# A planner's cost table changed: charges, a shared port and a settling time for chain matmuls

## The chip, the cores and the metric

The kernel runs on one core of one Trainium2 chip. The metric is the time of one execution on the device in microseconds. Before the change it is 2612.74 us, the median of 3 runs (2610.64 to 2614.07).

## The reference, cut to what matters

A stack of four layers works on 256 latent tokens and 256 context tokens of width 1024. A conditioning vector gives six modulation vectors to each layer. Each layer is a token mixer and then an MLP with squared ReLU (1024 to 4096 to 1024).

- Layers 0 and 3 mix by a gated DeltaNet with 8 heads in both directions: projections, a short convolution, then for each head and direction a triangular inverse and a recurrence over chunks, `o_c = qd_c S + attn_c v_new`, `S = S * cd + kt^T v_new`.
- Layer 1 mixes by a short gated convolution.
- Layer 2 mixes by differential attention with 8 heads: two softmaxes each, the second subtracted with a weight, then the product with v.
- The output is the latent stream after a last RMSNorm. Layer 3 finishes the latent tokens alone.

All is computed in float32. The projections and MLPs split each operand into a high and a low float32r part and add three products (high*high, high*low, low*high).

## The kernel before, in words

All instructions are issued by a planner, class `Issue`, while the program is built; nothing of it runs on the chip. Work is written as generators (`Strand`s). A strand yields either an `Op` (one instruction with its engine, its charge `cost` in ns and a latency `lat` until its result may be read) or a list of things that must be there first (a tile, a free PSUM bank, an event). `run` takes, over and over, the strand whose next step can start first by the planner's clocks (`start`), ties by priority, and `do` issues it: it moves the engine's clock by the charge and notes when the outputs can be read. So the charges set only the order of the instructions on each engine's queue, and in some places which of two engines does a copy (`evac` and `scaled` carry an alternative, `alt`). On the chip each engine runs its queue in that order and waits by semaphores.

Two sorts of matmul share TensorE. The projections' matmuls (`block`, `joint_prod`; kind float32r) read split weights (`whi`, `wlo`) and stream 256 or 512 columns; there are thousands of them, and in the long stretches of the MLPs nothing else runs on TensorE. The chains' matmuls are short: in the DeltaNet layers the transposes and norms of a head (`unit`, `turned`), the decays (`decays`, bf16), the inverse (`inverse`, float16, tile `Z`), the recurrence (`scan`, float32, tiles `S`, `rr`, `vk`, `vn`), and in attention the score, transpose and value products (`diff_probs`, `diff_head`). Between two matmuls of a chain stand VectorE, ScalarE or GpSimd steps. Chains have higher priority than projections, so that projections fill what the chains leave. PSUM has 3 banks for projections (`mm`), 4 for chains (`ch`) and one for outputs (`po`). Heads in flight are bounded by rings of buffers (`RINGS`: in layer 0 two buffers each of `E` and `NT`, in layer 3 three).

A matmul of a chain reaches the planner in one of two ways. The float32, bf16 and transpose ones are mostly yielded as `Op`s. The float16 ones of the inverse (`four`, `four_half`, `sums`), the products into `po` in `scan` and the attention scores are issued by `do` at once when the list before them is met.

During the DeltaNet layers GpSimd takes, beside its part in the chains, the low part of each weight (`splitter`, line 463).

Of the kernel before, what the change touches and what calls it, by code (L numbers as in the profile page):

```python
# [10 lines left out]
F32 = mybir.dt.float32  # L11
F32R = mybir.dt.float32r
F16 = mybir.dt.float16
BF16 = mybir.dt.bfloat16
# [4 lines left out]
PSUM = bass.MemoryType.PSUM  # L19
# [4 lines left out]
T = 256  # L24
TT = 2 * T
NB = TT // P
H = 8
# [4 lines left out]
DH = 64  # L32
LEVELS = 7
HALF = (slice(0, T), slice(T, TT))
LAT = dict(PE=197.0, ACT=150.0, DVE=145.0, POOL=80.0)
BIG = 1e18


class Op:

    __slots__ = ("eng", "cost", "outs", "ins", "emit", "lat", "func", "alt", "pre", "banks")

    def __init__(self, eng, cost, outs, ins, emit, lat, func=None):
        self.eng, self.cost, self.emit, self.lat, self.func, self.alt, self.pre = eng, cost, emit, lat, func, None, 0.0
        self.banks = [] if eng == "PE" else [a.name for a in ins + outs if a.space == PSUM]
        self.outs = [(a.name, Issue.buckets(a)) for a in outs]
        self.ins = [(a.name, Issue.buckets(a)) for a in ins]


class Strand:  # L50
    __slots__ = ("prio", "seq", "gen", "item", "r")
# [13 lines left out]
class Issue:  # L65
# [2 lines left out]

    TABLE = 1283.0
    AHEAD = 50.0  # L70

    def __init__(self, nc):
        self.nc = nc
        self.clk = dict(PE=0.0, ACT=0.0, DVE=0.0, POOL=0.0, DMA=0.0)
        self.rt, self.ft, self.birth, self.rings = {}, {}, {}, {}
        self.tasks, self.seq = [], 0
        self.n = 0
        self.held = set()
        self.loaded = None
        self.pe_begin = 0.0  # L80
        self.bank = {}


    def tile(self, pool, tag, shape, dt=F32, bufs=1, hold=False):
# [87 lines left out]
    def table(self, func):  # L172

        if TABLES[func] != self.loaded:
            self.loaded = TABLES[func]
            self.nc.scalar.preload_act_table_set(self.loaded)  # L176
            self.clk["ACT"] += self.TABLE

    def do(self, op):

        if op.alt is not None and self.clk[op.alt.eng] + op.alt.cost < self.clk[op.eng] + op.cost:
            op = op.alt
        eng = op.eng
        if self.swap_cost(op):
            self.table(op.func)
        begin = max(self.clk[eng], self.ready(op))
        if eng == "PE":
            begin = max(begin, self.pe_begin + op.pre)
            self.pe_begin = begin
        end = begin + op.cost  # L190
        self.clk[eng] = end
        for nm in op.banks:
            self.bank[nm] = (eng, end + op.lat)
        for nm, bs in op.ins:
            f = self.ft[nm]
            for b in bs:
                f[b] = max(f.get(b, 0.0), end)
        for nm, bs in op.outs:
            r = self.rt[nm]
            for b in bs:  # L200
                r[b] = end + op.lat
        op.emit()
# [9 lines left out]
    def mm(self, out, lhsT, rhs, start, stop, **k):  # L212
        n, m = self._n(rhs), self._n(lhsT)
        dt = lhsT.dtype
        if dt == F32R:
            c = n * 0.4167 + 3 if n >= 256 else 215
        elif dt == F32:
            c = n * 1.67 + 5 if n > 64 else 426
        else:
            c = n * 0.4167 + 2  # L220
        op = Op("PE", c, [out], [lhsT, rhs], lambda: self.nc.tensor.matmul(out, lhsT=lhsT, rhs=rhs, start=start, stop=stop, **k), LAT["PE"])  # L221
        op.pre = m * (0.84 if dt in (F32, F32R) else 0.21)
        if k and k["tile_position"][1]:
            op.cost, op.pre = 20, 0.0
        return op

    def transpose(self, out, in_, ident):
        op = Op("PE", 107, [out], [in_, ident], lambda: self.nc.tensor.transpose(out, in_, ident), LAT["PE"])  # L228
        op.pre = 53.0
        return op  # L230

    def act(self, out, in_, func, bias=0.0, scale=1.0, accum_out=None):
# [3 lines left out]
        return Op("ACT", c, [out] + ([accum_out] if accum_out is not None else []), [in_] + ptr,  # L236
                  lambda: self.nc.scalar.activation(out=out, in_=in_, func=func, bias=bias, scale=scale, **k), LAT["ACT"], func)  # L237

    def acopy(self, out, in_):
        return Op("ACT", self._n(in_) / 1.2 + (51 if self._ps(in_) else 93), [out], [in_],  # L240
                  lambda: self.nc.scalar.copy(out=out, in_=in_), LAT["ACT"])  # L241

    def vec(self, n, extra, outs, ins, emit, fast=False):
        ins = [x for x in ins if x is not None and not isinstance(x, float)]
        return Op("DVE", n / (1.92 if fast else 0.96) + extra, outs, ins, emit, LAT["DVE"])

    def vcopy(self, out, in_):
        return self.vec(self._n(in_), 68, [out], [in_], lambda: self.nc.vector.tensor_copy(out=out, in_=in_), not self._ps(in_, out))  # L248

    def vpred(self, out, mask, data):  # L250
        return self.vec(self._n(data), 68, [out], [data], lambda: self.nc.vector.copy_predicated(out=out, mask=mask, data=data))  # L251

    def vtt(self, out, in0, in1, op):
        return self.vec(self._n(in0), 68, [out], [in0, in1], lambda: self.nc.vector.tensor_tensor(out=out, in0=in0, in1=in1, op=op))  # L254
# [17 lines left out]
    def recip(self, out, in_):  # L272
        return Op("DVE", self._n(in_) * 6.3 + 68, [out], [in_], lambda: self.nc.vector.reciprocal(out=out, in_=in_), LAT["DVE"])

# [1 line left out]
        return Op("POOL", n * rate + extra, outs, ins, emit, LAT["POOL"])  # L276

    def ptt(self, out, in0, in1, op):
        return self.pool(self._n(in0), 2.2, 90, [out], [in0, in1],
                         lambda: self.nc.gpsimd.tensor_tensor(out=out, in0=in0, in1=in1, op=op))  # L280

    def psel(self, out, in_, pattern, compare_op, fill, base, cm):
# [17 lines left out]

    def load(self, out, in_):
        n = out.nbytes() if callable(out.nbytes) else out.nbytes
        self.do(Op("DMA", n / 330.0, [out], [], lambda: self.nc.sync.dma_start(out=out, in_=in_), 2000.0))

    def move(self, out, in_):

        n = out.nbytes() if callable(out.nbytes) else out.nbytes
        return Op("DMA", n / 330.0, [out], [in_], lambda: self.nc.sync.dma_start(out=out, in_=in_), 2000.0)


    def spawn(self, gen, prio):
# [27 lines left out]
    def start(self, e):  # L339

        op = e.item
        if not isinstance(op, Op):
            return max(e.r, self.clk["PE"] + self.AHEAD)
        t = self.clk[op.eng]
        if op.alt is not None:
            t = min(t, self.clk[op.alt.eng])
        if op.eng == "PE":
            t += self.AHEAD
        return max(e.r + self.swap_cost(op), t)

    def run(self):
# [23 lines left out]
class Net:  # L375
# [377 lines left out]
    def prod(self, ps, ah, al, bh, bl, first, last):  # L753
        mm = self.I.mm
        yield mm(ps, ah, bh, first, False)
        yield mm(ps, ah, bl, False, False)
        yield mm(ps, al, bh, False, last)
# [1029 lines left out]
```

## Time and profile before

| | |
|---|---|
| Median of 3 runs | 2612.74 us |
| The profiled execution | 2613.07 us, span 2611.4 us |
| TensorE matmul busy | 2515.1 us, 96% |
| TensorE weight load busy | 2091.5 us, 80% |
| VectorE, ScalarE, GpSimd busy | 1899.4, 1257.6, 389.3 us |
| HBM read | 317.44 MB |
| Mean granted clock of TensorE | 0.987 |

Matmuls are pipelined, and the profile models their ends. A busy TensorE can therefore hide short waits: the distance from one matmul's start to the next one's start tells more than the busy time.

### The profile page before, as it was taken

Reading aid. Unit: us, or ns where it says so; the run is one execution under the profiler, and the core shown is the slowest. Engines: PE = TensorE matmul, PEld = TensorE weight load, DVE = VectorE, ACT = ScalarE, POOL = GpSimd, SP = SyncE. Lnnn points to the kernel's source line nnn. Section 1 sums busy time; section 2 is a strip of 40 time slices with the busy share of each in tenths; the row PEclk is TensorE's granted clock in tenths of the full one; section 3 lists DMA queues with packets and bytes.
Section 4 is the critical chain, followed back from the end, with each engine's and each line's share of the span. In section 5 each row is a group of like instructions: output and inputs, shape, how many; then the busy total and the mean of one; then the engine's idle time right before and its main releaser. Section 6 shows DMA issues by size and latency. Waiting matters only on the chain. (4 is left out here: it accounts for less than half of the span.)

```text
span 2611.4 us, 41997 instructions
## 1 busy us (share of the span) xinstructions
PE 2515.1 (96%) x16396; PEld 2091.5 (80%) x16396; DVE 1899.4 (73%) x3499; ACT 1257.6 (48%) x2343; POOL 389.3 (15%) x273
## 2 busy tenths in 40 slices
PE   6999999899999999999999999999999999997998
PEld 3677777788888988888889666888888878786998
DVE  5776677699975645899856767799965787776665
ACT  4565565543333423533343544543333677765554
POOL 0444444200000000000000000000000254454000
PEclk9999999999999999999999999999999999998999
DMA  6312212456544133565532222365633111122564
GB/s 264 119 50 73 90 50 74 154 189 213 196 144 129 59 97 104 187 210 200 169 115 77 64 73 66 114 213 199 210 124 111 49 50 50 50 58 81 163 185 130
DMA packets 91638, 323.30 MB, mean 124 GB/s; under 512 B 10288, under 2 KB 13872, under 8 KB 91056
## 3 DMA queue, kind: packets, MB, share of 16 engines
q1 hardware_dynamic: 91440, 320.62, 37.8%
q8 instruction: 129, 2.11, 0.3%
q14 instruction: 69, 0.57, 0.1%
HBM read 317.44 MB, written 1.05 MB: 122 GB/s over the span
## 5 line engine op out<-in xcount | busy, mean ns | idle before, releaser
L241 ACT CAST whi<-raw 128x1024 fp32r<-128x1024 f32 x380 | 399.0, 1050 | 799.7 <-PE ch L221 431.9
L254 DVE TENSOR_TENSOR wlo<-raw,whi 128x1024 fp32r<-128x1024 f32 x305 | 374.2, 1227 | 236.6 <-ACT whi L241 236.3
L221 PE MATMUL mm<-hh,whi 128*128 128x512 f32 (+1 forms) x1344 | 490.2, 365 | 1.8 <-DVE x L257 1.1
L221 PE MATMUL mm<-hh,wlo 128*128 128x512 f32 (+1 forms) x1344 | 489.9, 364 | 0.8 <-DVE wlo L254 0.8
L221 PE MATMUL mm<-hl,whi 128*128 128x512 f32 (+1 forms) x1344 | 488.7, 364 | 0.0
L261 DVE CUSTOM_DVE_ANT_0 adaj<-adat,adas,pack 128x1024 bf16<-128x1024 f32 x288 | 368.5, 1280 | 8.5 <-ACT adas L237 5.7
L221 PE MATMUL ch<-hl,whi 128*128 128x512 f32 (+3 forms) x784 | 281.8, 359 | 5.9 <-DVE hl L257 5.9
L221 PE MATMUL ch<-u,whi 128*128 128x512 f32 (+1 forms) x1024 | 287.4, 367 | 0.0
L221 PEld LDWEIGHTS mm<-hh,whi 128*128 128x128 f32 x1344 | 257.8, 192 | 34.4 <-issue 7.7
L221 PEld LDWEIGHTS mm<-hh,wlo 128*128 128x128 f32 x1344 | 257.7, 192 | 32.8 <-issue 6.5
L221 PE MATMUL ch<-hh,whi 128*128 128x512 f32 (+3 forms) x784 | 281.5, 359 | 2.1 <-ACT hh L237 2.1
L221 PE MATMUL ch<-hh,wlo 128*128 128x512 f32 (+3 forms) x784 | 282.1, 360 | 0.0
L221 PEld LDWEIGHTS mm<-hl,whi 128*128 128x128 f32 x1344 | 257.8, 192 | 29.4 <-issue 4.7
L280 POOL TENSOR_TENSOR wlo<-raw,whi 128x1024 fp32r<-128x1024 f32 x75 | 182.0, 2429 | 284.5 <-ACT whi L241 279.6
L221 PE MATMUL mm<-u,whi 128*128 128x512 f32 (+1 forms) x768 | 215.6, 367 | 0.0
L221 PEld LDWEIGHTS ch<-u,whi 128*128 128x128 f32 x1024 | 183.6, 188 | 34.8
L221 PEld LDWEIGHTS <-Z 128*128 128x128 f16 x3072 | 141.0, 98 | 86.2 <-issue 50.2
L221 PE MATMUL ch<-u,wlo 128*128 128x512 f32 (+1 forms) x512 | 187.9, 367 | 0.0
L280 POOL TENSOR_TENSOR qk<-qk,rope 128x512 f32<-128x512 f32 x8 | 13.5, 1685 | 1104.2 <-DMA rt<-qk 1100.4
L221 PE MATMUL ch<-Z 128*128 128x64 f16 (+1 forms) x2816 | 173.0, 201 | 4.8 <-DVE Z L248 3.4
L257 DVE SCALAR_TENSOR_TENSOR x<-mm,mod,x 128x256 f32<-128x256 f32 x285 | 129.4, 479 | 63.7 <-PE mm L221 63.7
L251 DVE CAST_PREDICATED Z<-lev,ch 128x256 f16<-128x256 uint8 x384 | 143.2, 426 | 42.5 <-PE ch L221 40.6
(257 smaller groups left out, 4614.5 us busy)
## 6 DMA issues: line engine op xcount, KB each, us to landing
raw<-in_mlp_w SPq DMA_DIRECT2D x256, 512.0 KB, 3.6
adat<-in_ada_wT SPq DMA_DIRECT2D x144, 512.0 KB, 4.5
raw<-in_gdn_w_in SPq DMA_DIRECT2D x64, 512.0 KB, 3.7
adaw<-in_ada_w SPq DMA_DIRECT2D x48, 512.0 KB, 4.9
raw<-in_sconv_w_in SPq DMA_DIRECT2D x24, 512.0 KB, 3.6
raw<-in_diff_w_in SPq DMA_DIRECT2D x24, 512.0 KB, 3.7
raw<-in_gdn_w_out SPq DMA_DIRECT2D x16, 512.0 KB, 3.6
raw<-in_sconv_w_out SPq DMA_DIRECT2D x8, 512.0 KB, 3.5
```

Of the source, the lines that this page charges most:

```text
L221: op = Op("PE", c, [out], [lhsT, rhs], lambda: self.nc.tensor.matmul(out, lhsT=lhsT, rhs=rhs, start=start, stop=stop, **k), LAT["PE"])
L241: lambda: self.nc.scalar.copy(out=out, in_=in_), LAT["ACT"])
L251: return self.vec(self._n(data), 68, [out], [data], lambda: self.nc.vector.copy_predicated(out=out, mask=mask, data=data))
L254: return self.vec(self._n(in0), 68, [out], [in0, in1], lambda: self.nc.vector.tensor_tensor(out=out, in0=in0, in1=in1, op=op))
L257: return self.vec(self._n(in0), 130, [out], [in0, in1, scalar], lambda: self.nc.vector.scalar_tensor_tensor(out=out, in0=in0, scalar=scala ...
L261: return self.vec(self._n(in0), 130, [out, junk], [in0, in1, init], lambda: self.nc.vector.tensor_tensor_reduce(out=junk, in0=in0, in1=in1 ...
L280: lambda: self.nc.gpsimd.tensor_tensor(out=out, in0=in0, in1=in1, op=op))
```

## The change

It changes the planner's numbers and rules. No strand, tile or instruction is added or taken away, apart from which engine takes a copy that has an alternative.

- Latencies: PE 197 to 200, ACT 150 to 145, DVE 145 to 120, POOL 80 to 125 ns.
- Charges: a float32r matmul gets 14 instead of 3 ns beside its columns (115 for short ones); a predicated copy 130 instead of 68 ns; a GpSimd tensor_tensor 110 instead of 90; DMA 400 instead of 330 bytes per ns; the first of four 32-column matmuls 500.
- A port that GpSimd and VectorE share: an instruction of GpSimd, and one of VectorE with more than one SBUF input or in its fast mode, waits in the plan for the other engine's last one.
- A matmul's weight load starts in the plan only when its operands are ready, and a float32 or float32r one behind a float16, bf16 or transpose one gets 32 ns more.
- `SETTLE`: a yielded matmul that isn't float32r is taken 300 ns after its operands are ready by the plan, if another step can start before.

```diff
@@ -32,17 +32,20 @@
 DH = 64
 LEVELS = 7
 HALF = (slice(0, T), slice(T, TT))
-LAT = dict(PE=197.0, ACT=150.0, DVE=145.0, POOL=80.0)
+LAT = dict(PE=200.0, ACT=145.0, DVE=120.0, POOL=125.0)
 BIG = 1e18
 
 
 class Op:
 
-    __slots__ = ("eng", "cost", "outs", "ins", "emit", "lat", "func", "alt", "pre", "banks")
+    __slots__ = ("eng", "cost", "outs", "ins", "emit", "lat", "func", "alt", "pre", "banks", "port", "kind")
 
     def __init__(self, eng, cost, outs, ins, emit, lat, func=None):
-        self.eng, self.cost, self.emit, self.lat, self.func, self.alt, self.pre = eng, cost, emit, lat, func, None, 0.0
+        self.eng, self.cost, self.emit, self.lat, self.func, self.alt, self.pre, self.kind = eng, cost, emit, lat, func, None, 0.0, ""
         self.banks = [] if eng == "PE" else [a.name for a in ins + outs if a.space == PSUM]
+
+        big = [a for a in ins if a.space != PSUM and Issue._n(a) > 1]
+        self.port = eng == "POOL" or (eng == "DVE" and len(big) > 1)
         self.outs = [(a.name, Issue.buckets(a)) for a in outs]
         self.ins = [(a.name, Issue.buckets(a)) for a in ins]
 
@@ -68,6 +71,7 @@
 
     TABLE = 1283.0
     AHEAD = 50.0
+    SETTLE = 300.0
 
     def __init__(self, nc):
         self.nc = nc
@@ -77,8 +81,9 @@
         self.n = 0
         self.held = set()
         self.loaded = None
-        self.pe_begin = 0.0
+        self.pe_begin, self.pe_kind = 0.0, ""
         self.bank = {}
+        self.port = ("DVE", 0.0)
 
 
     def tile(self, pool, tag, shape, dt=F32, bufs=1, hold=False):
@@ -176,6 +181,13 @@
             self.nc.scalar.preload_act_table_set(self.loaded)
             self.clk["ACT"] += self.TABLE
 
+    def port_at(self, op):
+        return self.port[1] if op.port and self.port[0] != op.eng else 0.0
+
+    def change(self, op):
+
+        return 32.0 if op.pre > 50.0 and op.kind != self.pe_kind and self.pe_kind in ("H", "B", "T") else 0.0
+
     def do(self, op):
 
         if op.alt is not None and self.clk[op.alt.eng] + op.alt.cost < self.clk[op.eng] + op.cost:
@@ -183,10 +195,13 @@
         eng = op.eng
         if self.swap_cost(op):
             self.table(op.func)
-        begin = max(self.clk[eng], self.ready(op))
+        begin = max(self.clk[eng], self.ready(op), self.port_at(op))
+        if op.port:
+            self.port = (eng, begin + op.cost)
         if eng == "PE":
-            begin = max(begin, self.pe_begin + op.pre)
-            self.pe_begin = begin
+
+            begin = max(begin, max(self.pe_begin, self.ready(op)) + op.pre + self.change(op))
+            self.pe_begin, self.pe_kind = begin, op.kind
         end = begin + op.cost
         self.clk[eng] = end
         for nm in op.banks:
@@ -213,20 +228,21 @@
         n, m = self._n(rhs), self._n(lhsT)
         dt = lhsT.dtype
         if dt == F32R:
-            c = n * 0.4167 + 3 if n >= 256 else 215
+            c = n * 0.4167 + 14 if n >= 128 else 115
         elif dt == F32:
             c = n * 1.67 + 5 if n > 64 else 426
         else:
             c = n * 0.4167 + 2
         op = Op("PE", c, [out], [lhsT, rhs], lambda: self.nc.tensor.matmul(out, lhsT=lhsT, rhs=rhs, start=start, stop=stop, **k), LAT["PE"])
         op.pre = m * (0.84 if dt in (F32, F32R) else 0.21)
-        if k and k["tile_position"][1]:
-            op.cost, op.pre = 20, 0.0
+        op.kind = {F32: "F", F32R: "R", F16: "H", BF16: "B"}[dt]
+        if k and "tile_position" in k and m == 32:
+            op.cost, op.pre = (20, 0.0) if k["tile_position"][1] else (500, 107)
         return op
 
     def transpose(self, out, in_, ident):
         op = Op("PE", 107, [out], [in_, ident], lambda: self.nc.tensor.transpose(out, in_, ident), LAT["PE"])
-        op.pre = 53.0
+        op.pre, op.kind = 53.0, "T"
         return op
 
     def act(self, out, in_, func, bias=0.0, scale=1.0, accum_out=None):
@@ -242,13 +258,17 @@
 
     def vec(self, n, extra, outs, ins, emit, fast=False):
         ins = [x for x in ins if x is not None and not isinstance(x, float)]
-        return Op("DVE", n / (1.92 if fast else 0.96) + extra, outs, ins, emit, LAT["DVE"])
+        op = Op("DVE", n / (1.92 if fast else 0.96) + extra, outs, ins, emit, LAT["DVE"])
+        op.port |= fast
+        return op
 
     def vcopy(self, out, in_):
         return self.vec(self._n(in_), 68, [out], [in_], lambda: self.nc.vector.tensor_copy(out=out, in_=in_), not self._ps(in_, out))
 
     def vpred(self, out, mask, data):
-        return self.vec(self._n(data), 68, [out], [data], lambda: self.nc.vector.copy_predicated(out=out, mask=mask, data=data))
+        op = self.vec(self._n(data), 130, [out], [data], lambda: self.nc.vector.copy_predicated(out=out, mask=mask, data=data))
+        op.port |= not self._ps(data)
+        return op
 
     def vtt(self, out, in0, in1, op):
         return self.vec(self._n(in0), 68, [out], [in0, in1], lambda: self.nc.vector.tensor_tensor(out=out, in0=in0, in1=in1, op=op))
@@ -276,7 +296,7 @@
         return Op("POOL", n * rate + extra, outs, ins, emit, LAT["POOL"])
 
     def ptt(self, out, in0, in1, op):
-        return self.pool(self._n(in0), 2.2, 90, [out], [in0, in1],
+        return self.pool(self._n(in0), 2.2, 110, [out], [in0, in1],
                          lambda: self.nc.gpsimd.tensor_tensor(out=out, in0=in0, in1=in1, op=op))
 
     def psel(self, out, in_, pattern, compare_op, fill, base, cm):
@@ -300,12 +320,12 @@
 
     def load(self, out, in_):
         n = out.nbytes() if callable(out.nbytes) else out.nbytes
-        self.do(Op("DMA", n / 330.0, [out], [], lambda: self.nc.sync.dma_start(out=out, in_=in_), 2000.0))
+        self.do(Op("DMA", n / 400.0, [out], [], lambda: self.nc.sync.dma_start(out=out, in_=in_), 2000.0))
 
     def move(self, out, in_):
 
         n = out.nbytes() if callable(out.nbytes) else out.nbytes
-        return Op("DMA", n / 330.0, [out], [in_], lambda: self.nc.sync.dma_start(out=out, in_=in_), 2000.0)
+        return Op("DMA", n / 400.0, [out], [in_], lambda: self.nc.sync.dma_start(out=out, in_=in_), 2000.0)
 
 
     def spawn(self, gen, prio):
@@ -341,11 +361,14 @@
         op = e.item
         if not isinstance(op, Op):
             return max(e.r, self.clk["PE"] + self.AHEAD)
-        t = self.clk[op.eng]
+        t = max(self.clk[op.eng], self.port_at(op))
         if op.alt is not None:
             t = min(t, self.clk[op.alt.eng])
         if op.eng == "PE":
             t += self.AHEAD
+            if op.kind != "R":
+
+                t = max(t, e.r + self.SETTLE)
         return max(e.r + self.swap_cost(op), t)
 
     def run(self):
```

## Rows read from the trace of the kernel before

**Rows 1.** The page: busy time of an engine, share of the span, instructions.

```profile
PE 2515.1 (96%) x16396; PEld 2091.5 (80%) x16396; DVE 1899.4 (73%) x3499; ACT 1257.6 (48%) x2343; POOL 389.3 (15%) x273
PEclk9999999999999999999999999999999999998999
```

**Rows 2.** Windows: stretch, length, then busy us (instructions) of PE, PEld, DVE, ACT, POOL; clock, DMA.

```profile
65.00:470.00 405.00, 389.97 (x3451) 299.38 (x3451) 283.47 (x600) 245.41 (x548) 179.44 (x120) 1.00 0.25 79
650.00:700.00 50.00, 50.00 (x219) 40.76 (x218) 46.33 (x76) 16.05 (x21) 0.00 (x0) 1.00 0.59 200
1430.00:1640.00 210.00, 202.31 (x898) 140.69 (x897) 145.39 (x341) 97.75 (x217) 13.48 (x8) 1.00 0.24 73
2050.00:2385.00 335.00, 317.29 (x3162) 272.01 (x3161) 260.48 (x559) 237.03 (x531) 168.31 (x119) 0.98 0.19 56
2350.00:2385.00 35.00, 30.85 (x283) 29.56 (x283) 25.00 (x52) 20.31 (x36) 18.36 (x12) 0.90 0.19 54
```

**Rows 3.** Windows, PE alone, layer 0's mixer: matmuls with tile whi, wlo, Z in turn.

```profile
65.00:470.00 405.00, 189.51 (x519) 1.00 0.25 79
65.00:470.00 405.00, 111.02 (x260) 1.00 0.25 79
65.00:470.00 405.00, 91.87 (x1600) 1.00 0.25 79
```

**Rows 4.** Groups by form, PE, 65 to 470 us: busy us, mean ns, idle before.

```profile
L221 PE MATMUL ch<-Z 128*128 128x64 f16 x1088 | 52.3, 194 | 0.7 <-DVE Z L251 0.4
```

**Rows 5.** Timeline of PE at 388 us: start, length, matmul.

```profile
388.39 0.51 PE L221 MATMUL ch<-Z 128*128 128x64 f16 x12
388.74 0.48 PE L221 MATMUL mm<-hh,whi 128*128 128x512 f32 x1
389.06 0.39 PE L221 MATMUL mm<-hl,whi 128*128 128x512 f32 x1
```

**Rows 6.** Timeline of PE: first and last return to projections between 65 and 470.

```profile
66.86 0.48 PE L221 MATMUL ch<-hl,whi 128*128 128x512 f32 x1
67.18 0.40 PE L221 MATMUL ch<-hh,wlo 128*128 128x512 f32 x1
...
465.64 0.48 PE L221 MATMUL mm<-hh,whi 128*128 128x512 f32 x1
465.96 0.40 PE L221 MATMUL mm<-hl,whi 128*128 128x512 f32 x1
```

**Rows 7.** Timeline of PE at 2224 us (layer 3): a chain's matmul waits.

```profile
2224.14 0.39 PE L221 MATMUL mm<-hh,whi 128*128 128x512 f32 x1
2225.29 0.46 PE L221 MATMUL ch<-rr,NT 128*128 128x128 f32 x2 [0.76 <-DVE rr L257]
...
2225.81 0.39 PE L221 MATMUL ch<-Z 128*128 128x128 f16 x4
2226.00 0.48 PE L221 MATMUL mm<-hl,whi 128*128 128x512 f32 x1
2226.32 0.38 PE L221 MATMUL ch<-vk,kt 128*128 128x128 f32 x2
2226.54 0.28 PE L221 MATMUL ch<-S,u 128*128 128x128 f32 x1
```

**Rows 8.** Instructions on tile Z: ns min/median/max, first and last start.

```profile
L251 DVE CAST_PREDICATED Z<-lev,ch x384: 408/424/456, 98.0 to 2354.4; 128x256 f16<-128x256 uint8 x192
L251 DVE COPY_PREDICATED Z<-lev,Z x32: 677/1431/1762, 90.4 to 2335.5; 128x512 f16<-128x512 uint8 x32
L248 DVE CAST Z<-ident x23: 411/720/2550, 87.5 to 2334.1; 128x512 f16<-128x512 f32 x23
```

**Rows 9.** Timeline of all engines at 2300 us (layer 3).

```profile
2299.94 2.37 POOL L280 TENSOR_TENSOR wlo<-raw,whi 128x1024 fp32r<-128x1024 f32 x1
2300.04 2.55 DVE L248 CAST Z<-ident 128x512 f16<-128x512 f32 x1
...
2302.51 0.28 DVE L248 COPY S<-ch 128x128 f32<-128x128 f32 x1
...
2302.85 0.38 PE L221 MATMUL ch<-S,u 128*128 128x128 f32 x1 [1.79 <-DVE S L248]
```

**Rows 10.** Timeline of PE behind that wait.

```profile
2303.55 0.38 PE L221 MATMUL mm<-hh,wlo 128*128 128x256 f32 x1
2303.72 0.42 PE L221 MATMUL mm<-hh,whi 128*128 128x256 f32 x1
2303.93 0.42 PE L221 MATMUL mm<-hl,whi 128*128 128x256 f32 x1
```

## The prediction, made before the changed kernel ran

> **What bounds the kernel now.** I read the page's first part and its clock line first. TensorE is busy 96% of the span, at full clock almost everywhere [rows 1]. Since the ends of matmuls are modelled, I then asked the windows what a matmul really costs. In the first MLP, 219 matmuls of 512 columns take 50.00 us, 228 ns each, with no idle time [rows 2]; no order of the same matmuls can shorten such a stretch. What an order can change lies where chains share TensorE with projections: layer 0's mixer (65 to 470 us), attention (1430 to 1640) and layer 3's mixer (2050 to 2385). There TensorE is seen idle for 405 - 390.0 = 15.0, 210 - 202.3 = 7.7 and 335 - 317.3 = 17.7 us, 40.4 us in all [rows 2].
>
> More is hidden. I made a budget of starts for layer 0's mixer. Projections: 519 + 260 = 779 matmuls [rows 3] at 228 ns, 177.8 us. Float16: 1088 of 64 columns [rows 4] at (388.74 - 388.39)/12 = 29 ns [rows 5], 31.6 us; the other 1600 - 1088 = 512 at (2226.00 - 2225.81)/4 = 48 ns [rows 3, 7], 24.6 us. The remaining 3451 - 779 - 1600 = 1072 passes, most of them float32 of 128 columns, at (2226.54 - 2226.32)/2 = 110 ns [rows 2, 7], 117.9 us. The sum is 352 us of 405: 53 us are lost. 15.0 are the seen idle time. Another part is the price of going back to projections: the first one after a chain is followed by the next only after 0.32 us, 92 ns over the steady 228 [rows 5, 6]; the timeline has 181 such returns, the first and the last in [rows 6], 16.6 us. So 53 - 15 - 16.6 = about 22 us are short waits under modelled ends: weight loads and operands that come a little late. Scaled by the seen idle time (17.7/15.0), layer 3 has about 26 us of the same.
>
> **The change, part by part.** It moves only the order on the queues. The profiled execution took 2613.07 us (1.7 more than its span), 0.3 over the median of the three runs; I sum against it.
>
> Truer charges. The projection's charge goes from 216 to 227 ns against 228 measured [rows 2]. The predicated copy of 256 goes from 335 to 397 against a median of 424 [rows 8]; each of the inverse's levels has two in a row, so the plan had a level's result about 180 ns early and will have it 54 early. But the projections' clock ran early too, by 5%, so the two errors partly cancelled. By itself I take this for 0, bounded by 5 us both ways: the lost time in the float16 part is a share of the 22 us. The latencies move by 3 to 45 ns, less than a projection's matmul, and go with it. The charges for DMA and for the 32-column matmuls don't touch the bound stretches: loads come from SP's queue in the order of the plan, the DMA engines are busy 0.19 to 0.25 of those stretches [rows 2], and that slack hides a load that the new order puts later; without it a load would cost its own length on a projection.
>
> The shared port. The predicated copy from SBUF takes 677 ns at best and 1431 in the median, the cast of the identity 411 to 2550 [rows 8]. The worst shows what happens: GpSimd's low part of a weight runs from 2299.94 for 2.37 us, VectorE's cast starts at 2300.04 and lasts 2.55 us, and the 0.28 us copy of the state behind it in the queue comes at 2302.51; TensorE waits 1.79 us for that copy [rows 9]. Afterwards three matmuls of 256 columns stand 0.17 and 0.21 us apart [rows 10]; at the clock's lower level, 1.2 GHz, 256 columns are 0.213 us. That is part of layer 3's 0.98 [rows 2]. The old plan counted that cast as 335 ns; the new one sees that it can't run and takes the copy first, since an instruction that reads PSUM doesn't use the port. The bounds: 0 if the waits only change places; at most the idle time that something could have filled, 40.4 less the 4.2 of 2350 to 2385, where layer 3 runs out of projections [rows 2], so 36 us. In [rows 7] a projection stood ready at 2226.00 while TensorE idled 0.76 us, but not all waits are the port's. I take 14, including what settling does for waits over 0.3 us.
>
> Here a rule of the Trainium skill can be weighed: in "SBUF — State Buffer", section "Who interferes with whom", the one of GpSimd and VectorE that starts first holds the pair and the other is blocked fully, and issue order decides who blocks. The 2.55 us of [rows 9] agree with the block. But the plan's order of two engines isn't the chip's order when both are ready within some tens of ns; by that sentence taken strictly the plan's port would be right only part of the time, and the sum would lose the port's part, of which I count 10 of the 14 us: 2602 us, still inside the forecast's case, so it changes the size and not the sign.
>
> Settling. It acts on the float32, bf16 and transpose matmuls, and not on the float16 ones or the scores, which are issued at once. Such a matmul comes up to 300 ns later, behind one or two projections. What it saves is the wait of its weight load and operands: 0 at least, at most half of the 22 + 26 us of short waits, since the float16 matmuls keep theirs. I take 10, near the middle of 0 and 24.
>
> What settling costs. Queued behind the delayed matmul are projections that would have waited for it anyway; what waits for its result is the VectorE or ScalarE step of that chain, and then the PSUM bank, held up to 0.3 us longer. While projections remain this is hidden by them. Without that cover each of about 15 settled steps of a head (two transposes and two products before the inverse, eleven in the recurrence) costs one projection's 0.228 us at most, 3.4 us in a layer's last head, since the rule waits for nothing when there is no other work. Half of it in two layers is 3 us. What is late next, where a stall goes, is the same VectorE queue and then the 92 ns of each return, which stay.
>
> Sum: 2613 - 14 - 10 + 3 = 2592 us.
>
> **The rivals.**
>
> (a) Stalls change places. The budget is of starts, and the set of matmuls and returns stays; a projection taken earlier is one less filler later. For it: 16.6 us of the loss in layer 0 are returns that nothing removes, and half of TensorE's loss there isn't waiting that the profile shows. Against it: [rows 7] and [rows 9] show ready projections behind a waiting chain. Time: 2613, from 2608 to 2618.
>
> (b) Slower: the chains become the bound. Each head's 15 settled steps come about 0.3 us later, 4.5 us a head. With two heads in flight in layer 0 (two buffers of E and NT) the eight heads give 8 x 4.5/2 = 18 us, in layer 3 with three in flight 12 us. With 15 us of the gain left of the 24, this ends at 2613 + 30 - 15 = 2628 us, from 2618 to 2640. It decides from the point where projections run out before the chains do, as they do after 2350 us (4.2 us idle in 35, clock 0.90 [rows 2]); before that, GpSimd's 179 and VectorE's 283 of 405 us show slack in layer 0 [rows 2], which speaks against it.
>
> (c) Most of what can be filled is filled: 30 of the 36 us of seen idle and 18 of the 24 short waits, at 3 cost: 2568 us, from 2555 to 2578. For it, both examples had work ready; against it, waits like [rows 9] come from an in-order queue that a plan only estimates.
>
> **How the numbers follow.** The forecast has 0.48 (2578 to 2606), (c) 0.14, (a) 0.15, (b) 0.23. A measurement of this kernel can tell 0.2%, 5.2 us, from no change: below 2607.5 is faster, above 2618 slower. The forecast's case and (c) are faster, 0.62; (a) is the same, 0.15; (b) is slower, 0.23. The range from 2562 to 2624 leaves out the best of (c) and more than half of (b), under 2 in 10.
>
> **What would show it.** In the changed profile the MLP window still has 219 matmuls in 50 us. PE's idle time in the two mixers and attention falls from 40.4 to about 26 us, and in layer 3 the clock rises above 0.98. A cast of Z over 2 us has no PSUM copy queued behind it that TensorE waits for. Waits of TensorE for rr, S, kt and e shrink more than those for Z. The last projection of layer 0's mixer comes some 8 us earlier, of layer 3's some 10. I am wrong if the seen idle time stays at 40 us, if the mixers end no earlier, or if their end comes later with projections used up before the last head's recurrence; then (b) holds.

## The result: 2573.5 us, and the profile after

| | before | after |
|---|---|---|
| Median | 2611.96 us (4 runs, 2610.64 to 2614.07) | 2573.53 us (4 runs, 2572.81 to 2577.12) |
| Ratio | | 0.9854, 95% interval 0.9838 to 0.9869 |
| Profiled execution | 2613.07, span 2611.4 | 2573.83, span 2572.1 |

The change saves 38 us, 1.5%. The time lies in the range and on the side that was forecast, but in case (c), not in the forecast's own case. The page's first part after the change:

```profile
PE 2508.0 (98%) x16396; PEld 2090.8 (81%) x16396; DVE 1846.5 (72%) x3481; ACT 1252.0 (49%) x2349; POOL 389.1 (15%) x273
```

TensorE issues the same 16396 matmuls [rows 1]; VectorE is 53 us less busy with 18 instructions fewer. Now the windows of the changed kernel, with the columns of [rows 2]. The three shared stretches are cut at the same events as before: the first bound is moved by the 8 us that layer 0's chains start earlier, each other one by as much as the MLP behind the stretch starts earlier (13.6 us behind layer 0's mixer, 21.0 behind attention, 39.3 behind layer 3's), or the one in front.

```profile
57.00:457.00 400.00, 395.08 (x3469) 304.73 (x3468) 276.42 (x615) 248.18 (x546) 181.96 (x120) 1.00 0.25 79
650.00:700.00 50.00, 50.00 (x220) 40.82 (x218) 48.63 (x78) 16.07 (x21) 0.00 (x0) 1.00 0.66 218
1417.00:1619.00 202.00, 198.33 (x886) 140.54 (x885) 135.66 (x332) 102.09 (x224) 14.00 (x8) 1.00 0.25 74
2029.00:2346.00 317.00, 308.14 (x3136) 267.25 (x3136) 238.62 (x534) 227.42 (x537) 172.26 (x122) 0.99 0.21 63
```

The MLP is what it was: 220 matmuls in 50 us. The stretches are 400, 202 and 317 us long, 919 instead of 950, and TensorE is seen idle for 4.9, 3.7 and 8.9 us, 17.5 instead of 40.4 [rows 2]. So 31 of the 38 us come from the shared stretches: 23 were idle time that the profile shows, and 8 are busy time. What those 8 are isn't shown: waits hidden under modelled ends are one part, but layer 3's clock also rose from 0.98 to 0.99, by the rounded figures an estimated 0.02 x 335 - 0.01 x 317 = 3.5 us, and the three windows hold 20 matmuls fewer (7491 against 7511). The other 8 lie ahead of layer 0's chains, which start that much earlier; the experiment on charges below says what that was worth.

Who TensorE waited for, in layer 0's mixer and in layer 3's, first before and then after (us in total, times, longest):

```profile
PE ch L221 <- DVE Z L251: 5.4, 6, 1.4
PE ch L221 <- DVE Z L248: 3.4, 2, 1.7
PE ch L221 <- DVE rr L257: 1.5, 1, 1.5
...
PE ch L221 <- DVE o L254: 5.0, 3, 2.5
PE ch L221 <- DVE Z L251: 3.4, 4, 1.6
PE ch L221 <- DVE S L248: 1.8, 1, 1.8
PE ch L221 <- DVE S L257: 1.0, 1, 1.0
```

```profile
PE ch L236 <- DVE Z L269: 2.4, 3, 1.6
PE ch L236 <- DVE abg L266: 1.7, 1, 1.7
...
PE ch L236 <- POOL Z L300: 3.1, 1, 3.1
PE ch L236 <- DVE Z L269: 1.9, 3, 1.5
```

The reader is to see that most waits before were for VectorE (13.8 of 14.7 us in layer 0, 13.7 of 17.0 in layer 3), and that those for the recurrence (`rr`, `S`) and for the normed output `o` are gone but for one of 0.3 us, while those for the inverse's `Z` are fewer but not gone. The longest wait after the change is a new one: 3.1 us for GpSimd's product on `Z`, which stood in GpSimd's queue behind the 2.57 us low part of a weight and two products on `o`. VectorE's held instructions on Z, to be read against [rows 8]:

```profile
L269 DVE COPY_PREDICATED Z<-lev,Z x32: 678/1084/1756, 82.8 to 2311.9; 128x512 f16<-128x512 uint8 x32
L266 DVE CAST Z<-ident x20: 411/534/2594, 81.7 to 2299.8; 128x512 f16<-128x512 f32 x20
```

The medians fall from 1431 to 1084 and from 720 to 534 ns, but a cast of 2.6 us is still there. It shows that the plan doesn't know the order on the chip. Timeline of all engines around it:

```profile
2080.25 3.17 DVE L266 CAST Z<-ident 128x512 f16<-128x512 f32 x2
...
2080.59 5.08 POOL L300 TENSOR_TENSOR wlo<-raw,whi 128x1024 fp32r<-128x1024 f32 x2
...
2083.34 0.77 DVE L269 CAST_PREDICATED Z<-lev,ch 128x256 f16<-128x256 uint8 x2
2083.83 0.25 PE L236 MATMUL ch<-Z 128*128 128x64 f16 x3 [1.55 <-DVE Z L269]
```

GpSimd got in 0.24 us ahead of the second cast, two PSUM copies stood behind that cast, and TensorE idled 1.55 us. It is the picture of [rows 9] again.

### The profile page after: what moved, and what is told of

Its sections match the earlier page's. It is cut to its first block, busy times and chain, and to the rows that moved or that the text cites. A ratio compares the mean times of both kernels' runs of the same rounds, so it can differ in the third digit from the quotient of the medians.

```text
span 2572.1 us, 41962 instructions
## 1 busy us (share of the span) xinstructions
PE 2508.0 (98%) x16396; PEld 2090.8 (81%) x16396; DVE 1846.5 (72%) x3481; ACT 1252.0 (49%) x2349; POOL 389.1 (15%) x273
## 5 line engine op out<-in xcount | busy, mean ns | idle before, releaser
L236 PEld LDWEIGHTS <-Z 128*128 128x128 f16 x3072 | 147.3, 97 | 78.0 <-issue 43.9
```

## The experiments

Each kernel was timed in 3 rounds against the kernel before, which measured 2610.6 to 2613.1 us beside them; ratios carry the 95% interval.

| kernel | port in the plan | median us | ratio |
|---|---|---|---|
| the change without settling | yes | 2597.87 | 0.9945 (0.9930 to 0.9959) |
| the change without the port | no | 2617.68 | 1.0017 (1.0007 to 1.0026) |
| the change without the weight-load rule | yes | 2575.01 | 0.9854 (0.9839 to 0.9869) |
| the change with the old charges | yes | 2564.39 | 0.9816 (0.9802 to 0.9831) |
| port alone | yes | 2575.38 | 0.9862 (0.9847 to 0.9877) |
| settling alone | no | 2606.34 | 0.9983 (0.9973 to 0.9992) |
| port and settling | yes | 2566.92 | 0.9830 (0.9815 to 0.9844) |
| the change, nudged | yes | 2587.15 | 0.9907 (0.9891 to 0.9924) |
| before, nudged | no | 2621.64 | 1.0043 (1.0028 to 1.0058) |
| port and settling, nudged | yes | 2574.21 | 0.9853 (0.9836 to 0.9871) |
| port alone, in clocks only | yes | 2585.86 | 0.9905 (0.9891 to 0.9920) |
| port and settling, copies too | yes | 2578.69 | 0.9880 (0.9866 to 0.9895) |

My theory at the start: port and settling each take waits away and are worth 8 to 14 us each; the charges set the earlier start; the weight-load rule is worth little. Rivals: one part is all of it, or any new order falls somewhere by chance.

**Without the port**

```diff
     def port_at(self, op):
-        return self.port[1] if op.port and self.port[0] != op.eng else 0.0
+        return 0.0
```

> The changed kernel without the shared port in the plan; all else stays. Theory: 8 to 14 us come back, 2582 to 2588 us, and casts of Z that GpSimd holds over 2 us again have PSUM copies behind them for which TensorE waits. Rival 1 (settling alone covers such waits): 2571 to 2577. Rival 2 (chance of the order): 2564 to 2584 without those waits.

It gave back 44 us, three times what the theory said, and is slower than the kernel before. Its windows in layer 0, attention and layer 3:

```profile
57.00:472.00 415.00, 397.69 (x3486) 304.85 (x3484) 296.36 (x627) 247.71 (x539) 186.31 (x121) 1.00 0.24 78
1432.00:1645.00 213.00, 203.46 (x884) 141.51 (x883) 139.04 (x334) 98.97 (x221) 13.37 (x8) 0.98 0.23 70
2054.00:2389.00 335.00, 316.87 (x3158) 271.12 (x3156) 259.74 (x561) 236.20 (x529) 171.28 (x121) 0.98 0.19 58
```

The idle time is back: 17.3, 9.5 and 18.1 us, a little more than in [rows 2]. With the other three parts in place, the plan that doesn't see the port has all the old waits.

**Port alone**

The kernel before, with the changed kernel's lines for `op.port`, `self.port` and `port_at`, and nothing else.

> The kernel before with the shared port in its plan and nothing else: no settling, old weight-load rule, old charges. Taking the port out of the change cost 44 us, taking settling out 24, together more than the change's 38. Theory (port and settling need each other: a plan that doesn't see the port has late results however long it waits, and a plan without settling takes a chain's matmul too early): port alone gains 10 to 20 us, 2593 to 2603. Rival 1 (the port is the whole gain and settling only mends what the charges spoil): 2565 to 2585. Rival 2 (each part only reshuffles): 2605 to 2620.

Rival 1 holds: 2575.4 us, a gain of 36 us, as much as the whole change within 2 us. Its windows:

```profile
61.00:456.00 395.00, 391.65 (x3468) 299.88 (x3468) 276.60 (x615) 243.94 (x542) 183.01 (x120) 1.00 0.27 84
1416.00:1622.00 206.00, 199.71 (x902) 141.42 (x901) 142.64 (x340) 97.80 (x219) 13.18 (x8) 1.00 0.25 75
2032.00:2347.00 315.00, 309.17 (x3158) 265.42 (x3158) 240.43 (x539) 229.22 (x539) 166.21 (x119) 1.00 0.20 60
```

Idle: 3.4, 6.3 and 5.8 us. The two mixers are as clean as with the whole change, and attention, where GpSimd does 13 us of work in all, keeps most of its idle time.

**Settling: taken out, and alone**

```diff
-            if op.kind != "R":
-                t = max(t, e.r + self.SETTLE)
```

> The changed kernel without the settling rule: a chain's matmul is taken again as soon as its operands are ready by the plan; charges, port and weight-load rule stay. Theory (each part takes its own waits away): settling saved the short waits of the float32, bf16 and transpose matmuls, so about 10 to 14 us come back, 2584 to 2588 us, and TensorE's seen idle time in the three shared stretches grows. Rival 1 (the charges and the port did it, settling is nothing): 2571 to 2577. Rival 2 (any new order falls by chance somewhere within 10 us): 2564 to 2584 with no growth in the waits of just these matmuls.

> The kernel before with the settling rule alone. Theory: within 5 us of the kernel before, 2608 to 2618, because waits behind GpSimd's hold on the port are up to 2.5 us and 0.3 us of settling doesn't cover them. Rival 1 (settling is a cause by itself): 2588 to 2603, with layer 0 and attention shorter as its removal made them longer. Rival 2 (it costs where the port isn't seen): 2620 or more.

Taken out of the change it costs 24 us; added to the kernel before it gains 5, a ratio of 0.9983. Neither is what I expected: the first is more than 14, the second lies 2 us below the 2608 I gave. The windows without it, in layer 0, attention and layer 3:

```profile
54.00:472.00 418.00, 406.32 (x3481) 308.40 (x3483) 281.76 (x614) 253.90 (x552) 182.43 (x120) 0.99 0.24 77
1432.00:1642.00 210.00, 201.99 (x895) 140.02 (x894) 146.83 (x341) 98.70 (x218) 14.00 (x8) 1.00 0.24 73
2052.00:2370.00 318.00, 311.60 (x3126) 265.86 (x3125) 245.94 (x537) 223.94 (x526) 167.75 (x121) 1.00 0.20 60
```

Layer 0 is 18 us longer than after the change (it begins 3 us earlier) and 11.7 us idle instead of 4.9; attention is 8 us longer and 8.0 us idle instead of 3.7; layer 3 is 1 us longer with less idle time, 6.4 us.

**Port and settling, and the two other parts**

Port and settling together on the kernel before, with the old charges and the old weight-load rule:

> Port and settling alone on the kernel before: old charges, old weight-load rule. Theory: these two are the whole gain, so 2560 to 2578 us. Rival (the weight-load rule replaced the truer charges where they were taken out, 2564 us): 2585 or more.

The change with the old charges, and the change with the old weight-load rule (`begin = max(begin, self.pe_begin + op.pre)`):

> The changed kernel with all old charges and latencies (projections 216 ns, predicated copies 335, DMA 330 bytes per ns, 32-column matmuls, latencies), but with port, weight-load rule and settling. Theory: the first DeltaNet chains start some 8 us later again, as in the kernel before (first matmul on Z at 92 instead of 84 us), and the rest is within 5 us: 2579 to 2587 us. Rival (charges are the main cause): 2590 or more. Rival (the charges are nothing, the start is another part's): 2571 to 2576.

> The changed kernel with the old rule for weight loads (behind the last matmul's start only, no 32 ns for a change of kind). Theory: worth little by itself, 2571 to 2579 us, since 107 ns on a chain's matmul is less than one projection's 228 ns. Rival (truer clock of TensorE is the cause of the gain): 2585 or more.

Port and settling are enough: 2566.9 us. The weight-load rule moves nothing in the sum (2575.0 against 2573.5), but by two moves that cancel: with the old rule layer 0's mixer ends at 446 instead of 457 us, and layer 3's takes 326 instead of 317 us.

```profile
54.00:446.00 392.00, 387.26 (x3466) 300.16 (x3465) 276.31 (x615) 246.17 (x544) 181.73 (x120) 1.00 0.26 82
2018.00:2344.00 326.00, 308.94 (x3144) 266.65 (x3143) 255.28 (x549) 225.49 (x527) 162.05 (x119) 0.98 0.19 56
```

The old charges in the change make it 9 us faster, 2564.4, the fastest kernel here; none of the three expectations had that. One half of the theory held, the start of layer 0's chains. First and last start of the inverse's first matmul in layer 0, before, after, and after with the old charges:

```profile
L221 PE MATMUL ch<-ident,Z x64: 217/220/315, 92.1 to 422.2; 128*128 128x128 f16 x64
```

```profile
L236 PE MATMUL ch<-ident,Z x64: 217/219/233, 84.2 to 413.4; 128*128 128x128 f16 x64
```

```profile
L236 PE MATMUL ch<-ident,Z x64: 218/219/231, 94.2 to 413.2; 128*128 128x128 f16 x64
```

With the old charges the chains start at 94.2 instead of 84.2 us and yet end at the same 413 us. So the charges bring the start forward by 10 us, and it is worth nothing: what starts earlier waits later. The 9 us between the two kernels lie in layer 3's mixer.

**How far a shuffle moves the time**

Three kernels with two numbers moved a little, for no reason (in the kernel before only the second):

```diff
-    SETTLE = 300.0
+    SETTLE = 310.0
-    AHEAD = 50.0
+    AHEAD = 55.0
```

> The changed kernel with two numbers moved by a little: settling 310 instead of 300 ns, projections taken 55 instead of 50 ns ahead. It tells how far the time moves when the order is shuffled without a reason: some 1400 lines of TensorE's queue differ, where the parts' removal changed 3500 to 4100. Theory: the parts' differences of 24 and 44 us are causes, and the shuffle moves 2573.5 by no more than 6 us. Rival (chance of the order makes differences of 10 us and more): outside 2564 to 2584.

> The kernel before with projections taken 55 instead of 50 ns ahead: a shuffle of the order without a reason and without the port. The same kind of nudge moved the changed kernel by 13.6 us, all of it in layer 3's mixer. Theory (the port's 36 to 44 us are a cause, and the scatter of orders is some 15 us): 2596 to 2626 us. Rival (the kernel before is an unlucky order, and most orders are near 2575): 2590 or less.

> Port and settling alone, nudged (settling 310, 55 ns ahead). Theory: the plan that sees the port stays 25 us and more under the kernel before, whatever the shuffle: 2555 to 2587 us. Rival (2566.9 was luck): 2590 or more.

They moved by +13.6, +11.0 and +7.3 us. My 6 us for the first was far too small. Where the 13.6 went: layer 3's mixer alone (2029 to 2359 us, 330 instead of 317), with TensorE's waits there:

```profile
2029.00:2359.00 330.00, 312.88 (x3133) 269.62 (x3133) 254.15 (x538) 229.97 (x535) 170.41 (x122) 0.97 0.20 60
```

```profile
PE ch L236 <- DVE Z L269: 4.4, 6, 1.7
PE ch L236 <- ACT Z L257: 4.1, 4, 3.3
PE ch L236 <- POOL Z L300: 2.4, 2, 1.9
PE ch L236 <- DVE rr L277: 1.7, 1, 1.7
```

Idle time is 17.1 us there instead of 8.9, in 20 waits instead of 12, the longest of 1.7 to 3.3 us, and the clock is 0.97 instead of 0.99. I take a handful of such waits, met or missed, for the scatter of orders: some 7 to 14 us. All three nudges made the time longer and all three carry the same 55, so a cost of that number itself isn't ruled out.

Against the scatter stand the kernels sorted by the port. The four plans without it lie between 2606 and 2622 us, the ten with it, the change among them, between 2564 and 2598; the two sets don't meet. The port gained 36, 39 and 44 us in three pairs of kernels that differ in it alone. So its gain is shown, and its size to within the scatter.

Settling made the time shorter in each of three pairs (5, 8.5 and 24 us). How much of that is scatter can be told in attention, where the nudges move little: from the last matmul of layer 1's MLP to the first of the second product in layer 2's MLP they moved the time by 0.1 to 0.8 us, while settling shortened it from 341.3 to 337.9, from 337.8 to 334.9 and from 340.5 to 333.1 us. Some 3 to 7 us of settling are shown there; what it does in the mixers, and the charges and the weight-load rule, are not told from the scatter.

**What the port does: other work for VectorE, or true times for all**

```diff
-        t = max(self.clk[op.eng], self.port_at(op))
+        t = self.clk[op.eng]
```

in `start`, on port alone: the clocks still count the hold, the choice of the next step doesn't look at it.

> Port alone, but only in the planner's clocks: an instruction still counts as held for the time when its result can be read, yet the choice of what comes next doesn't look at the port, so VectorE's queue isn't put in another order on its account. Theory (as the prediction put it: the gain is that VectorE does other work while GpSimd holds the port): most of port alone's 36 us go, 2595 to 2615. Rival (the gain is that consumers, TensorE first, are told the true time and take something else meanwhile): 2565 to 2587.

The time is the rival's: 2585.9 us, so 25 of the 36 us are there although the choice of the next step doesn't look at the port. VectorE's held instructions on Z, busy us and mean ns, in port alone and then in this kernel:

```profile
L269 DVE COPY_PREDICATED Z<-lev,Z 128x512 f16<-128x512 uint8 x32 | 37.4, 1173 | 1.1 <-ACT Z L257 1.1
L266 DVE CAST Z<-ident 128x512 f16<-128x512 f32 x22 | 16.8, 766 | 0.0
```

```profile
L269 DVE COPY_PREDICATED Z<-lev,Z 128x512 f16<-128x512 uint8 x32 | 40.9, 1285 | 2.1 <-ACT Z L257 2.0
L266 DVE CAST Z<-ident 128x512 f16<-128x512 f32 x21 | 18.6, 888 | 0.0
```

The same two in the kernel before:

```profile
L251 DVE COPY_PREDICATED Z<-lev,Z 128x512 f16<-128x512 uint8 x32 | 42.2, 1328 | 0.1
L248 DVE CAST Z<-ident 128x512 f16<-128x512 f32 x23 | 20.5, 903 | 0.0
```

In clocks only they are held about as long as before (1285 and 888 ns against 1328 and 903), and the gain is there all the same. It is so for all of VectorE's work: the instructions that ran over 1 us longer than the shortest of the same operation, tiles and shape in any kernel here are 36 before, 34 in clocks only and 18 in port alone, and each of them overlaps one of GpSimd. So most of the gain doesn't need shorter holds. That those who wait for these results are put in the queue later is the reading that is left; the queues themselves weren't compared, and one more thing changed: 22 instructions went from VectorE to ScalarE (3477 and 2365 against 3499 and 2343), as the choice of a copy's engine reads a clock that counts the hold. The windows of clocks only show where the gain lies:

```profile
67.00:455.00 388.00, 386.18 (x3448) 297.65 (x3451) 271.73 (x600) 248.85 (x547) 179.39 (x119) 1.00 0.26 81
1415.00:1621.00 206.00, 200.87 (x904) 141.23 (x903) 139.26 (x336) 102.05 (x224) 13.62 (x8) 1.00 0.25 75
2031.00:2358.00 327.00, 311.18 (x3144) 270.13 (x3143) 251.71 (x534) 239.36 (x547) 171.63 (x122) 0.98 0.20 59
```

Idle time is 1.8, 5.1 and 15.8 us. Layer 0 and attention are as clean as in port alone, but layer 3 is idle almost as long as before, 327 us long against 335 before and 315 in port alone. So the 10.5 us between the two kernels are layer 3's: there the choice by the port may count, or it is the scatter, which moved just this stage by 13 us above.

**A port for the copies, too**

```diff
-        if op.alt is not None and self.clk[op.alt.eng] + op.alt.cost < self.clk[op.eng] + op.cost:
+        if op.alt is not None and max(self.clk[op.alt.eng], self.port_at(op.alt)) + op.alt.cost < self.clk[op.eng] + op.cost:
```

and the same in `start`, on port and settling.

> Port and settling alone, and the choice between ScalarE and VectorE for a copy looks at the port too, so that a cast from SBUF goes to ScalarE while GpSimd holds the port. Theory: fewer long casts on VectorE, 3 to 10 us under port and settling's 2566.9: 2556 to 2564. Rival (ScalarE's queue is late already, or these casts no longer set anything): 2564 to 2580, the scatter of orders.

The theory fell. The edit did what it was meant to, VectorE's casts of the identity are 10 instead of 24, but the time is 2578.7 us, 12 us more than port and settling, a step that the scatter covers. The fastest kernel stays the change with the old charges, 0.9816 of the time before; it is 2.5 us under port and settling and no more than the scatter under the change.

## Why the prediction was right, and where its sizes were off

- **What bounds the kernel.** Right. All of the stretches that hold nothing but projections kept their time; layer 1 and the end are the same within 1 us, and the gain is in the two mixers and attention.
- **Truer charges, 0 within 5 us.** Not confirmed. With port and settling in place they made the time 9 us longer beside the new weight-load rule (2573.5 against 2564.4) and 8 us longer beside the old one (2575.0 against 2566.9), more than 5 but within the scatter. Together they bring layer 0's chains forward by 10 us, which I hadn't seen (which of them does it wasn't tried), and nothing comes of it.
- **The shared port, 14 us.** This term was mis-sized: alone it is worth 36 us. Its upper bound, the idle time that something could fill, was 36 us, and I took less than half of it since not all waits looked like the port's. The runs show that most were: the idle time of the three stretches is 40.4 us before, 45 without the port in the changed plan, and 15.5 with the port alone. That the gain equals the bound is chance, though: 25 of the 36 us are idle time, the rest is busy time and an earlier start. The mechanism was off as well. I said that VectorE would take the copy behind the held cast first; that choice is some 10 of the 36 us, all in layer 3, if it isn't scatter. The greater part is there without it. Plan times that no longer promise results up to 2.2 us early ([rows 9]: 2.55 us against a charge of 335 ns), so that TensorE's queue has projections where a chain's matmul would have stood waiting, fit this, but that step is argued and not shown.
- **The rule of the Trainium skill** that I weighed ("SBUF — State Buffer", section "Who interferes with whom"), on who gets the port first, came true in part: GpSimd's instruction began 0.24 us ahead of the cast at 2080.8 us, which was then held for 2.6 us in a plan that sees the port. It didn't cost the port's term.
- **Settling, 10 us, at a cost of 3.** The sign is right in three pairs, and 8.5 us on top of the port is near the 7 that I took, though by the scatter that nearness may be luck. The same rule taken out of the whole change costs 24: 15 us in layer 0, which I can't tell from the scatter of orders, 8 in attention and 1 in layer 3.
- **Hidden short waits.** Not shown. Beside 23 us of idle time 8 us of busy time went, near the 10 forecast, but part of that may be the clock and the cut of the windows. One price of the budget was low, too: the 48 ns of a float16 matmul of 128 columns came from one place [rows 7], and in layer 0 the median is 56 ns, which makes the 22 us of hidden waits 18.
- **Rivals.** (a) falls: stalls did not change places. (b) falls: the chains are no bound, since layer 3's mixer is shorter and TensorE less idle. (c) has the time, 2573.5 us in 2555 to 2578, and the reason that I gave for it, ready work behind the waits, but not the sum: 23 us of idle time went instead of 30, at most 8 of short waits instead of 18, and 8 us are an earlier start that no case had. It had 0.14, too little for a case whose bound the rows gave as 36 us.
- **What would show it.** The MLP window, the fall of idle time (17.5, forecast 26), the clock in layer 3 (0.99) and the waits for `rr` and `S` came as said. The mixers gave back more than the 8 and 10 us said: layer 0's ends 13.6 us earlier, and layer 3's is 18 us shorter. Two signs did not come: that no long cast has a PSUM copy behind it, and that the waits for `e` shrink (3.0 us in attention, before and after).

What stays open: settling's size in the mixers, whether the truer charges cost anything, and by which step the later plan times shorten TensorE's waits. Telling them from the scatter would take many orders of each kind, not more rounds of one.

## What to carry to other kernels

A plan that puts out queues in order must know of every resource that two engines share; one such hold left out was worth more than all the durations corrected beside it. Where the order is made by a greedy plan, nudge a number that should not matter before believing a gain of half a per cent: here such nudges moved the time by 7 to 14 us. And when a bound from the rows (the idle time that ready work could fill) is far above the value taken, say by name which waits are to be left out; here 25 of 40 us were the port's.
